# A hybrid retention and sliding-window decoder layer on one core: 28 more 128x512 tiles turned by DMA transposes of two 16-bit planes, in buffers of their own

## The chip, the cores and the metric

One NeuronCore of a Trainium2 chip runs the whole layer in one launch. The metric is the device time of that launch in microseconds (us), the median of several runs. All matrix products are 32-bit: TensorE (PE) takes each fp32 weight tile as a high part and a low part in its reduced fp32 format, and three products make one.

## The reference

The layer is computed for 256 positions of width 2048.

```python
h = modulate(rms_norm(x, norm_ffn1), mod0, mod1)
x = x + 0.5 * mod2 * swiglu(h, w_ffn1_gu, w_ffn1_down)          # d_ff 5632
h = modulate(rms_norm(x, norm_mix), mod3, mod4)
rq, rk, rv, rg, sq, sk, sv, gl_ret, gl_swa = split(h @ w_in)     # 13312 columns
ro = group_rms(retention(rotary(rq), rotary(rk), rv))            # 8 heads, 128 / 256
y_ret = (silu(rg) * ro) @ w_ret_branch
y_swa = sliding_window_attention_with_sinks(sq, sk, sv) @ w_swa_branch   # 32 / 8 heads of 64
x = x + mod5 * ((sigmoid(gl_ret) * y_ret + sigmoid(gl_swa) * y_swa) @ w_out)
h = modulate(rms_norm(x, norm_ffn2), mod6, mod7)
x = x + 0.5 * mod8 * swiglu(h, w_ffn2_gu, w_ffn2_down)
out = rms_norm(x, norm_final)
```

The nine `mod` vectors are `silu(c) @ w_ada + b_ada`, 2048 by 18432 weights that VectorE (DVE) multiplies row by row beside the products ("ada passes", L204).

## The kernel before, in words

Activations are held turned, features on the 128 partitions and the 256 positions along the row, because PE multiplies from that form. A product (`gemm`, L385) makes a chunk of 512 output columns for both halves of the positions in two PSUM banks. It streams the weights in loads of 1 MB (`load`, L309, four buffers in the pool `raws`); each load holds four 128-row blocks and is worked off in two halves. For each half ScalarE (ACT) casts the high part `wh` (L335), DVE subtracts to get the low part `wl` (L336), into a pool of three such pairs, and PE issues twelve 128x512 matmuls (L327, L328, L329). A chunk of a 2048-row product is four loads, eight halves, 96 matmuls.

After each load of a chunk `step` (L300) runs one step of the first generator in the list `side`: a pair of heads of the softmax (`window`, L1000, weights in one step and values in the next) or a head of the retention (L1059). So the softmax and the retention run between the products of the following chunks.

A result of a product has the positions on the partitions. Where a later product needs it, each 128x512 tile of it must be turned. There are two ways in the kernel:

- `transpose_to` (L412): four 128x128 transposes on PE into one PSUM bank (L417) and one copy out of it (L418), by ACT or DVE as the scheduler chooses.
- `turn_by_dma` (L424), which only the feed-forward chunks use, 8 tiles in the first and 20 in the second: ACT copies the low and the high 16 bits of each word apart into two planes (`apart`, L432, two copies), SyncE (SP) issues two DMA transposes (`turn`, L436), and two copies weave the turned planes together (`together`, L442). Planes and turned planes share one tile of the pool `asp` (tile name `a`, two buffers), which the softmax and the products' activation pairs use too. `later` (L552) gives these out over the following loads: the first tile's `apart`, the second's, three empty steps, the first `turn`, the second, then both `together`.

The middle part of the layer, which the change is about, goes in this order: keys and values of the softmax; four chunks of softmax queries (L1012 on, turned into `qo`); two chunks each of rotated queries and keys (L1026 on, into `qk`); four chunks of retention values; the gates of the first half; four chunks of gated retention (L1122 on, into `rot`); then for each half `p` of the columns the two branch products, whose gated sum is turned into `mt` (L1137 on).

SP is the one engine whose order is that of the code: it issues the loads, the ada rows and the DMA transposes in the order in which the kernel calls them, each waiting until its buffer is free. On PE, DVE and ACT a scheduler sets the order when the program is built, and the engine then keeps to it, whatever comes late.

Of the kernel before, what the change touches and what calls it, by code (L numbers as in the profile page):

```python
# [11 lines left out]
U16 = mybir.dt.uint16  # L12
# [5 lines left out]
P = 128  # L18
# [6 lines left out]
CH = 512  # L25
KB = 4
# [51 lines left out]
def layer_kernel(  # L78
# [22 lines left out]
    nc = tc.nc  # L101
# [15 lines left out]
    def nm(s):  # L117
        uid[0] += 1
        return f"{s}_{uid[0]}"
# [7 lines left out]
    def side_bank():  # L127
        return psd.tile([P, CH], F32, tag="pd", name=nm("pd"))
# [7 lines left out]
    def slot():  # L136
        return slots.tile([P, KD * S], F32, tag="slot", name=nm("slot"))
# [201 lines left out]
    def pair_tile():  # L339
        return asp.tile([P, 2, CH], F32, tag="a", name=nm("a"))  # L340
# [42 lines left out]

    def gemm(act, w, col0s, KT=KD):
        banks = [[acc_bank() for _ in range(NT)] for _ in col0s]  # L385
# [27 lines left out]
    def transpose_to(dest, src_of, n, ps=None):  # L413

        ps = ps or bank()
        for j in range(n):
            nc.tensor.transpose(ps[:, j * P : (j + 1) * P], src_of(j), ident)  # L417
        nc.any.tensor_copy(dest, ps[:, : n * P])  # L418

    def words(t):  # L420

        return t.bitcast(U16).rearrange("p (n i) -> p n i", i=2)

    def turn_by_dma(dest, src):  # L424


        both = pair_tile()
        planes = both[:, 0].bitcast(U16).rearrange("p (i n) -> p i n", i=2)
        turned = both[:, 1].bitcast(U16).rearrange("p (i k s) -> p i k s", i=2, k=KB)
        def apart():  # L430
            for i in range(2):
                nc.scalar.copy(planes[:, i, :], words(src)[:, :, i])  # L432

        def turn():
            for i in range(2):
                nc.sync.dma_start_transpose(turned[:, i], planes[:, i, :])  # L436

        into = dest.bitcast(U16).rearrange("p k (s i) -> p k s i", i=2)

        def together():  # L440
            for i in range(2):
                nc.any.tensor_copy(into[:, :, :, i], turned[:, i])  # L442

        return apart, turn, together

# [103 lines left out]
        square_sum(ssq[:, t * 4 + ci : t * 4 + ci + 1], xs)  # L549


    def later(work):  # L552
# [6 lines left out]
        m1()  # L559

    def swiglu_up(banks_g, banks_u, tiles, ci, parts=None, by_dma=False):

        k0 = ci * KB
        dest = tiles[k0 // KD].rearrange("p (k s) -> p k s", s=S)
        kk = k0 % KD
        work = []
        for t in range(NT):
            s = t512()
            g, u = banks_g[t], banks_u[t]
            if parts is not None:  # L570
                nc.vector.tensor_add(s, g, parts[0][t])
                nc.vector.tensor_add(parts[1][t], u, parts[1][t])
                g, u = s, parts[1][t]
            nc.scalar.activation(s, g, AF.Silu)
            nc.vector.tensor_mul(s, s, u)
            if by_dma:
                work.append(turn_by_dma(dest[:, kk : kk + KB, t * P : (t + 1) * P], s))
                continue
            transpose_to(
                dest[:, kk : kk + KB, t * P : (t + 1) * P],  # L580
                lambda j: s[:, j * P : (j + 1) * P],
                KB,
            )
        if work:
            side.append(later(work))

    def ffn_up(held, w, tiles, first, bg=None, turned=()):
        for ci in range(first, DFF // CH):
# [148 lines left out]
    held = Held()  # L737
# [138 lines left out]
    def in_chunk(c0):  # L876
        return gemm(held, wi, [c0])[0]
# [123 lines left out]
    def window(pair):  # L1001
        lg = window_weights(pair)
        yield
        if before:
            window_values(*before.pop())
        before.append((pair, lg))
        if pair == QH // 2 - 1:
            yield
            window_values(*before.pop())
        yield  # L1010

    for ci in range(4):  # L1012
# [12 lines left out]
    qk = slot().rearrange("p (a h s) -> p a h s", a=2, h=RH)  # L1025
    for a, off in ((0, O_RQ), (1, O_RK)):  # L1026
        for ci in range(2):
            b = in_chunk(off + ci * CH)
            for t in range(NT):
# [20 lines left out]
                transpose_to(  # L1050
                    qk[:, a, ci * 4 : ci * 4 + 4, t * P : (t + 1) * P],
                    lambda j: u[:, j * P : (j + 1) * P],
                    4,
                )


    vo = slot().rearrange("p (t n) -> p t n", t=NT)

    def retention(h):  # L1059
        ps = side_bank()  # L1060
        nc.tensor.matmul(
            ps[:, :S], qk[:, 1, h, :P], qk[:, 0, h, :], start=True, stop=True
# [58 lines left out]
    rot = slot().rearrange("p (k s) -> p k s", s=S)  # L1121
    for ci in range(4):  # L1122
        b = in_chunk(O_RG + ci * CH)
        for t in range(NT):
# [3 lines left out]
            transpose_to(  # L1128
                rot[:, ci * 4 : ci * 4 + 4, t * P : (t + 1) * P],
                lambda j: u[:, j * P : (j + 1) * P],  # L1130
                4,
            )

    gate = gate_row()
    mt = slot().rearrange("p (k s) -> p k s", s=S)
# [2 lines left out]
    for p in range(2):  # L1138
        sg = first if p == 0 else gates(p)
        c0s = [(2 * p + i) * CH for i in range(2)]  # L1140
        for g, a, w in ((1, a_swa, w_swa_branch), (0, a_ret, w_ret_branch)):
            banks = gemm(a, w[0], c0s)
            for i in range(2):
                for t in range(NT):
                    nc.vector.tensor_mul(sg[:, g, i, t, :], sg[:, g, i, t, :], banks[i][t])
        for i in range(2):
            for t in range(NT):
                m = sg[:, 0, i, t, :]
                nc.vector.tensor_add(m, m, sg[:, 1, i, t, :])
                k0 = (2 * p + i) * KB  # L1150
                transpose_to(
                    mt[:, k0 : k0 + KB, t * P : (t + 1) * P],
                    lambda j: m[:, j * P : (j + 1) * P],
                    KB,
                )
# [94 lines left out]
```

## Time and profile before

| | |
|---|---|
| median of 3 runs | 2430.84 us (2430.41 to 2431.67) |
| span of the profiled execution, first to last instruction | 2429.6 us |
| what lies around the span, against the median | 1.2 us |
| PE busy | 2385.2 us, 98% |
| DVE busy | 1701.3 us, 70% |
| ACT busy | 1236.0 us, 51% |
| DMA queue q1 | 597.91 MB, 70.8% of the engines' time |
| granted TensorE clock | 0.999 |

The span is one profiled execution; PE, DVE, ACT and SP are engines, PEld is PE's weight load, SPq is SP's queue of DMA issues. A group row gives line, engine, operation, output and inputs by tile name, shape, count, then busy us and mean ns, then the idle time before and what ended it. A matmul row's length contains its latency; how much of PE it takes is read from the starts of the rows that follow each other. The middle part that the change touches stands between about 850 and 1440 us.

### The profile page before, as it was taken

The page shows a single profiled execution, that of the slowest core. Times are in us where ns is not written, and L with a number is a line of the kernel's source. Part 1 is how long each engine was busy: PE and PEld are TensorE (multiplying, and loading weights), DVE is VectorE, ACT ScalarE, POOL GpSimd, SP SyncE. Part 2 cuts the span into 40 slices and gives each one's busy share as a digit, 9 for nine tenths or more (in the row PEclk, how much of TensorE's full clock was granted, in tenths as well). Part 3 has the DMA queues.
Part 4 walks back from the last instruction along what each step waited for, and adds up shares of the span by engine and source line. Part 5 has one row for each costly group of instructions (what it writes and reads, how often), then busy time and mean ns, then how long its engine had stood idle before and what let it go on. Part 6 is the DMA issues. An engine that isn't in the chain of part 4 may idle for free. (4 is left out here: it accounts for less than half of the span.)

```text
span 2429.6 us, 29064 instructions
## 1 busy us (share of the span) xinstructions
PE 2385.2 (98%) x10798; PEld 1946.8 (80%) x10798; DVE 1701.3 (70%) x2735; ACT 1236.0 (51%) x1696; POOL 5.7 (0%) x14
## 2 busy tenths in 40 slices
PE   7999999999999999999999999999999999999998
PEld 4778888888787777788888888887788888888886
DVE  6998777778877677886666776767655555555656
ACT  6544545454545455554544444446554555554544
POOL 0000000000000000000000000000000000000000
PEclk9999999999999999999999999999999999999999
DMA  9987689998875665566676777755677777775563
GB/s 347 341 333 284 217 313 318 356 319 295 311 264 186 243 222 204 206 219 216 233 266 245 251 260 260 279 189 190 215 249 237 243 251 238 248 237 192 185 198 122
DMA packets 274545, 606.43 MB, mean 250 GB/s; under 512 B 40098, under 2 KB 40482, under 8 KB 255586
## 3 DMA queue, kind: packets, MB, share of 16 engines
q1 hardware_dynamic: 272898, 597.91, 70.8%
q0 software_dynamic: 928, 5.61, 0.6%
q8 instruction: 85, 1.39, 0.2%
q10 hardware_dynamic: 576, 1.05, 0.1%
q14 instruction: 58, 0.47, 0.1%
HBM read 595.06 MB, written 2.12 MB: 246 GB/s over the span
## 5 line engine op out<-in xcount | busy, mean ns | idle before, releaser
L336 DVE TENSOR_TENSOR wl<-raw,wh 128x1024 fp32r<-128x1024 f32 (+1 forms) x828 | 995.9, 1208 | 591.2 <-ACT wh L335 585.3
L335 ACT CAST wh<-raw 128x1024 fp32r<-128x1024 f32 (+1 forms) x828 | 861.4, 1042 | 973.0 <-PE pa L328 936.8
L327 PE MATMUL pa<-wh,hh 128*128 128x512 f32 x2224 | 870.5, 393 | 3.4 <-ACT wh L335 2.9
L328 PE MATMUL pa<-wh,hl 128*128 128x512 f32 x2224 | 869.9, 391 | 2.2 <-DVE hl L503 1.8
L329 PE MATMUL pa<-wl,hh 128*128 128x512 f32 x2224 | 798.0, 392 | 4.0 <-DVE wl L336 4.0
L327 PEld LDWEIGHTS pa<-wh,hh 128*128 128x128 f32 x2224 | 418.1, 188 | 93.4 <-ACT wh L335 4.4
L329 PEld LDWEIGHTS pa<-wl,hh 128*128 128x128 f32 x2224 | 415.9, 188 | 95.9 <-DVE wl L336 9.8
L328 PEld LDWEIGHTS pa<-wh,hl 128*128 128x128 f32 x2224 | 418.3, 188 | 89.8 <-DVE hl L503 2.5
L328 PE MATMUL pa<-wh,a 128*128 128x512 f32 x992 | 383.9, 389 | 0.0
L327 PE MATMUL pa<-wh,a 128*128 128x512 f32 x992 | 367.1, 390 | 1.6 <-DVE t L546 1.2
L329 PE MATMUL pa<-wl,a 128*128 128x512 f32 x992 | 367.1, 390 | 0.8 <-DVE wl L336 0.8
L327 PEld LDWEIGHTS pa<-wh,a 128*128 128x128 f32 x992 | 186.1, 188 | 41.5 <-DVE t L546 1.9
L329 PEld LDWEIGHTS pa<-wl,a 128*128 128x128 f32 x992 | 185.9, 188 | 40.6 <-DVE wl L336 2.4
L328 PEld LDWEIGHTS pa<-wh,a 128*128 128x128 f32 x992 | 186.3, 188 | 38.5
L204 DVE CUSTOM_DVE_ANT_0 slot<-slot,cact 128x512 f32<-128x512 f32 (+1 forms) x252 | 192.8, 814 | 10.5 <-DMA slot<-in_w_ada_dram 10.3
L204 DVE CUSTOM_DVE_ANT_0 raw<-raw,cact 128x512 f32<-128x512 f32 (+1 forms) x260 | 167.1, 696 | 42.5 <-DMA raw<-in_w_ada_dram 32.3
L368 DVE TENSOR_TENSOR a<-slot,a 128x512 fp32r<-128x512 f32 x124 | 85.0, 686 | 13.2 <-ACT a L367 13.2
L367 ACT CAST a<-slot 128x512 fp32r<-128x512 f32 x124 | 76.4, 616 | 14.8 <-PE pa L329 14.7
L442 ACT COPY slot<-a 128x512 uint16<-128x512 uint16 x54 | 38.5, 772 | 31.3 <-DMA a<-a 31.3
L204 DVE DVE_READ_ACCUMULATOR2_ANT sums<- 128x1 f32 x512 | 42.4, 83 | 0.0
L418 ACT COPY slot<-ps 128x512 f32<-128x512 f32 x52 | 29.4, 584 | 23.7 <-PE ps L417 23.5
L462 ACT ACTIVATE pd<-x_sb 128x512 f32<-128x512 f32 x32 | 19.0, 593 | 34.6 <-DVE x_sb L547 32.1
(164 smaller groups left out, 1024.2 us busy)
## 6 DMA issues: line engine op xcount, KB each, us to landing
raw<-in_w_ffn_gu_dram SPq DMA_DIRECT2D x152, 1024.0 KB, 5.2
raw<-in_w_in_dram SPq DMA_DIRECT2D x104, 1024.0 KB, 5.0
raw<-in_w_ffn_down_dram SPq DMA_DIRECT2D x88, 1024.0 KB, 5.1
slot<-in_w_ada_dram SPq DMA_DIRECT2D x76, 1024.0 KB, 7.3
raw<-in_w_ada_dram SPq DMA_DIRECT2D x64, 1024.0 KB, 4.8
raw<-in_w_ffn_gu_dram SPq DMA_DIRECT2D x24, 768.0 KB, 6.9
raw<-in_w_swa_branch_dram SPq DMA_DIRECT2D x16, 1024.0 KB, 5.3
raw<-in_w_ret_branch_dram SPq DMA_DIRECT2D x16, 1024.0 KB, 5.1
```

What stands on the lines that cost most here:

```text
L204: nc.vector.tensor_tensor_reduce(out=w[:, at], in0=w[:, at], in1=cact[:, at], scale=1.0, scalar=0.0, op0=ALU.mult, op1=ALU.add, accum_out= ...
L327: nc.tensor.matmul(ps, ah[:, j, ts], wh[:, j, :], start=first, stop=False)
L328: nc.tensor.matmul(ps, al[:, j, ts], wh[:, j, :], start=False, stop=False)
L329: nc.tensor.matmul(ps, ah[:, j, ts], wl[:, j, :], start=False, stop=last)
L335: nc.scalar.copy(hi, src)
L336: nc.vector.tensor_sub(lo, src, hi.bitcast(F32))
L367: nc.scalar.copy(hi, v)
L368: nc.vector.tensor_sub(lo, v, hi.bitcast(F32))
L418: nc.any.tensor_copy(dest, ps[:, : n * P])
L442: nc.any.tensor_copy(into[:, :, :, i], turned[:, i])
L462: nc.scalar.activation(side_bank(), src, AF.Square, accum_out=dest)
```

## The change

Tiles are turned by `turn_by_dma` in 28 more places instead of by `transpose_to`: the 8 tiles of the softmax queries, the 8 of rotated queries and keys, the 8 of gated retention and the 4 of the merged branches of the first half `p = 0`. The second half stays on PE. The planes and the turned planes get two pools of their own, `flat` (4 buffers of 2 KB a partition) and `back` (2 of 2 KB), and are taken when they are written. The scratch space of the GpSimd queue's DMAs is set to 4096 bytes. Turns move out of `side` into a list of their own, `turns`: after each load every generator in it makes one step. The softmax pairs of a chunk are put into `side` only when its tiles are together, eight loads after the chunk's end. In the code behind it, lines stand 15 to 33 further down: the products L327 to L329 become L342 to L344, the cast L335 becomes L350, the load L312 becomes L327, the ada row L199 becomes L201, the weaving copies L442 become L461.

```diff
+    flat = ctx.enter_context(tc.tile_pool(name="flat", bufs=4))
+    back = ctx.enter_context(tc.tile_pool(name="back", bufs=2))
...
+    turns = []
+    def turn_step():
+        for one_turn in list(turns):
+            if next(one_turn, turns) is turns:
+                turns.remove(one_turn)
+    def soon(one_turn):
+        next(one_turn)
+        turns.append(one_turn)
...
     def gemm_part(act, w, col0s, banks, kb, KT):
...
                 tick()
+            turn_step()
...
     def turn_by_dma(dest, src):
-        both = pair_tile()
-        planes = both[:, 0].bitcast(U16).rearrange("p (i n) -> p i n", i=2)
-        turned = both[:, 1].bitcast(U16).rearrange("p (i k s) -> p i k s", i=2, k=KB)
+        held = {}
         def apart():
+            planes = flat.tile([P, 2, CH], U16, tag="flat", name=nm("flat"))
             for i in range(2):
                 nc.scalar.copy(planes[:, i, :], words(src)[:, :, i])
+            held["planes"] = planes
         def turn():
+            turned = back.tile([P, 2, KB, P], U16, tag="back", name=nm("back"))
             for i in range(2):
-                nc.sync.dma_start_transpose(turned[:, i], planes[:, i, :])
+                nc.sync.dma_start_transpose(turned[:, i], held["planes"][:, i, :])
+            held["turned"] = turned
...
+    def later_by_pairs(work):
+        for apart, _, _ in work:
+            apart()
+        for _ in range(5):
+            yield
+        for a in range(0, len(work), 2):
+            for which in (1, 2):
+                yield
+                for parts in work[a : a + 2]:
+                    parts[which]()
...
     for ci in range(4):
         b = in_chunk(O_SQ + ci * CH)
+        work = []
         for t in range(NT):
             u = t512()
             nc.any.tensor_copy(u, b[t])
-            transpose_to(
-                qo[:, ci * 4 : ci * 4 + 4, t * P : (t + 1) * P],
-                lambda j: u[:, j * P : (j + 1) * P],
-                4,
-            )
-        side += [window(pair) for pair in range(ci * 4, ci * 4 + 4)]
+            work.append(turn_by_dma(qo[:, ci * 4 : ci * 4 + 4, t * P : (t + 1) * P], u))
+        pairs = range(ci * 4, ci * 4 + 4)
+        soon(later(work, lambda pairs=pairs: side.extend(window(pair) for pair in pairs)))
```

The rotated queries and keys and the gated retention change in the same way, with `soon(later(work))`; the merged branches use `soon(later_by_pairs(work))`.

On PE the place is the first chunk of rotated keys, second load. Before, the four transposes of a tile of rotated queries (`t_7822`, into the bank `ps_7829`) stand between the products of that chunk (`pa_7848` and `pa_7849` are its two banks):

```order
L327 MATMUL pa_7848<-wh_7916,hh_4122 128x512
L328 MATMUL pa_7848<-wh_7916,hl_4123 128x512
L329 MATMUL pa_7848<-wl_7917,hh_4122 128x512
L327 MATMUL pa_7849<-wh_7916,hh_4122 128x512
L417 MATMUL ps_7829<-small_c,t_7822 128x128 x4
L328 MATMUL pa_7849<-wh_7916,hl_4123 128x512
L329 MATMUL pa_7849<-wl_7917,hh_4122 128x512
L327 MATMUL pa_7848<-wh_7935,hh_4122 128x512
L328 MATMUL pa_7848<-wh_7935,hl_4123 128x512
```

Now, at the same load of that chunk (banks `pa_7693` and `pa_7694`):

```order
L344 MATMUL pa_7693<-wl_7756,hh_4136 128x512
L344 MATMUL pa_7694<-wl_7756,hh_4136 128x512
L342 MATMUL pa_7693<-wh_7755,hh_4136 128x512
L343 MATMUL pa_7693<-wh_7755,hl_4137 128x512
L344 MATMUL pa_7693<-wl_7756,hh_4136 128x512
L342 MATMUL pa_7694<-wh_7755,hh_4136 128x512
L343 MATMUL pa_7694<-wh_7755,hl_4137 128x512
L344 MATMUL pa_7694<-wl_7756,hh_4136 128x512
L342 MATMUL pa_7693<-wh_7774,hh_4136 128x512
```

The transposes are gone from PE and the products follow each other.

On SP the place is the loads of the second chunk of rotated keys (`raw` from `in_w_in`) with the ada rows between them. Before:

```order
L312 DMA raw_8119<-in_w_in_dram 128x4x512
L199 DMA raw_8137<-in_w_ada_dram 128x2048
L312 DMA raw_8186<-in_w_in_dram 128x4x512
L312 DMA raw_8241<-in_w_in_dram 128x4x512
L199 DMA raw_8276<-in_w_ada_dram 128x2048
L312 DMA raw_8308<-in_w_in_dram 128x4x512
```

Now (`flat_7730` and `flat_7793` hold the planes of the two tiles of rotated queries, `back_8064` and `back_8137` take them turned):

```order
L327 DMA raw_7968<-in_w_in_dram 128x4x512
L201 DMA raw_7986<-in_w_ada_dram 128x2048
L327 DMA raw_8029<-in_w_in_dram 128x4x512
L454 DMA_TRANSPOSE back_8064<-flat_7730 128x4x128 x2
L327 DMA raw_8099<-in_w_in_dram 128x4x512
L201 DMA raw_8134<-in_w_ada_dram 128x2048
L454 DMA_TRANSPOSE back_8137<-flat_7793 128x4x128 x2
L327 DMA raw_8160<-in_w_in_dram 128x4x512
```

Two pairs of transposes now stand between the loads; the loads and ada rows keep their order.

On ACT the place is the same tile's way into `qk`. Before, one copy out of PSUM (`slot_7305` is `qk`) stands among the casts and the softmax's copies:

```order
L335 CAST wh_7916<-raw_7914 128x1024
L418 COPY t_7802<-ps_7803 128x384
L418 COPY t_7808<-ps_7809 128x384
L335 CAST wh_7935<-raw_7914 128x1024
L335 CAST wh_7973<-raw_7971 128x1024
L997 COPY slot_6378<-ps_7814 128x256
L418 COPY slot_7305<-ps_7829 128x4x128
L335 CAST wh_7990<-raw_7971 128x1024
```

Now (`slot_7142` is `qk`; the other of the two weaving copies of this tile stands on DVE, and its two `apart` copies stand a few rows further up):

```order
L350 CAST wh_7844<-raw_7825 128x1024
L989 ACTIVATE a_7796,sm_7814<-a_7796,ng_7809 128x128 x2
L989 ACTIVATE a_7796,sm_7814<-a_7796,ng_7809 128x256 x2
L1030 COPY slot_6392<-ps_7745 128x256
L983 ACTIVATE se_7811<-se_7811 128x4
L350 CAST wh_7886<-raw_7884 128x1024
L461 COPY slot_7142<-back_8064 128x4x128
L350 CAST wh_7903<-raw_7884 128x1024
L350 CAST wh_7970<-raw_7968 128x1024
L434 COPY t_7864<-ps_7865 128x384
L434 COPY t_7870<-ps_7871 128x384
L350 CAST wh_7989<-raw_7968 128x1024
```

The copy that waited for PE is replaced by a copy that waits for a transfer, one cast behind the cast `wh_7844` of the load whose buffer `raw_8029` takes (the fourth `raw` back on SP).

More of the change, by code (lines that the diff above doesn't have):

```diff
@@ L441, in together @@
             for i in range(2):
-                nc.any.tensor_copy(into[:, :, :, i], turned[:, i])
+                nc.any.tensor_copy(into[:, :, :, i], held["turned"][:, i])
         return apart, turn, together
@@ L549, in add_gated, with later @@
         square_sum(ssq[:, t * 4 + ci : t * 4 + ci + 1], xs)
-    def later(work):
+    def later(work, then=None):
         (a0, t0, m0), (a1, t1, m1) = work
@@ L559, in later @@
         m1()
+        if then is not None:
+            then()
+    def later_by_pairs(work):
[8 more added lines that the diff above has]
+                    parts[which]()
     def swiglu_up(banks_g, banks_u, tiles, ci, parts=None, by_dma=False):
@@ L584, in swiglu_up @@
         if work:
-            side.append(later(work))
+            turns.append(later(work))
     def ffn_up(held, w, tiles, first, bg=None, turned=()):
@@ L1028, in layer_kernel @@
             b = in_chunk(off + ci * CH)
+            work = []
             for t in range(NT):
@@ L1049, in layer_kernel @@
                 nc.vector.tensor_add(u4[:, :, 1, :], u4[:, :, 1, :], v4[:, :, 1, :])
[L1050 to L1053, printed above, removed]
+                work.append(
+                    turn_by_dma(qk[:, a, ci * 4 : ci * 4 + 4, t * P : (t + 1) * P], u)
                 )
+            soon(later(work, lambda heads=(a, ci): kept.add(heads)))
     vo = slot().rearrange("p (t n) -> p t n", t=NT)
     def retention(h):
+        assert {(0, h // 4), (1, h // 4)} <= kept
         ps = side_bank()
@@ L1123, in layer_kernel @@
         b = in_chunk(O_RG + ci * CH)
+        work = []
         for t in range(NT):
@@ L1127, in layer_kernel @@
             nc.vector.tensor_mul(u, u, vo[:, t, ci * CH : (ci + 1) * CH])
[L1128 to L1132, printed above, removed]
+            work.append(turn_by_dma(rot[:, ci * 4 : ci * 4 + 4, t * P : (t + 1) * P], u))
+        soon(later(work))
     gate = gate_row()
@@ L1141, in layer_kernel @@
         for g, a, w in ((1, a_swa, w_swa_branch), (0, a_ret, w_ret_branch)):
+            assert g == 1 or not turns
             banks = gemm(a, w[0], c0s)
@@ L1145, in layer_kernel @@
                     nc.vector.tensor_mul(sg[:, g, i, t, :], sg[:, g, i, t, :], banks[i][t])
+        work = []
         for i in range(2):
@@ L1150, in layer_kernel @@
                 k0 = (2 * p + i) * KB
[L1151 to L1155, printed above, removed]
+                dest = mt[:, k0 : k0 + KB, t * P : (t + 1) * P]
+                if p == 0:
+                    work.append(turn_by_dma(dest, m))
+                    continue
+                transpose_to(dest, lambda j: m[:, j * P : (j + 1) * P], KB)
+        if work:
+            soon(later_by_pairs(work))
     gate_load(gate, 5)
@@ L1227 @@
     from concourse.bass_utils import run_bass_kernel_spmd as _run
[L1229 removed]
+    nc = _bacc.Bacc("TRN2", target_bir_lowering=False, num_devices=1, dynamic_dma_scratch_size=4096)
     arrays, args = {}, []
```

2 lines of the change are left out of this document (1 added, 1 removed).

## The prediction

> **What bounds the kernel now.** I read the page's busy times and slices first, then three stretches, then the starts of single rows on PE, ACT and SP, and last what ACT waited for.
>
> ```profile
> PE 2385.2 (98%) x10798; PEld 1946.8 (80%) x10798; DVE 1701.3 (70%) x2735; ACT 1236.0 (51%) x1696; POOL 5.7 (0%) x14
> ...
> PEclk9999999999999999999999999999999999999999
> ```
>
> PE works 98% of the span at the full granted clock, so whatever leaves PE's queue leaves the time, as long as PE stays fed. The stretches show where it is fed (columns: us; busy us and count on PE, PEld, DVE, ACT, POOL; clock; DMA share; GB/s):
>
> ```profile
> 875.00:1110.00 235.00, 235.00 (x1283) 187.03 (x1282) 181.47 (x410) 132.42 (x282) 0.00 (x0) 1.00 0.59 206
> 1190.00:1430.00 240.00, 239.25 (x1073) 197.30 (x1073) 162.36 (x245) 113.74 (x129) 0.00 (x0) 1.00 0.72 255
> 1760.00:2180.00 420.00, 420.00 (x1855) 347.77 (x1854) 235.67 (x285) 214.05 (x251) 1.59 (x3) 1.00 0.76 241
> ```
>
> The first is the softmax with the queries and keys, the second the gated retention and the first branches, both touched by the change. The third is the second feed-forward, which turns its tiles by transfer already: 1855 matmuls in 420.00 us, 0.2264 us each, which is a matmul's bare pitch (below). So **PE lost nothing there to 19 turned tiles** (38 transposes, two a tile). All three stretches are bound by PE; a busy PE can hide pauses of up to the 0.16 us by which a row is longer than its pitch, so the terms below come from starts.
>
> **The change, part by part: what leaves PE.** A tile's four transposes between two products:
>
> ```profile
> 886.77 0.40 PE L328 MATMUL pa<-wh,hl 128*128 128x512 f32 x1
> 887.00 0.39 PE L329 MATMUL pa<-wl,hh 128*128 128x512 f32 x1
> 887.23 0.40 PE L327 MATMUL pa<-wh,hh 128*128 128x512 f32 x1
> 887.46 0.39 PE L328 MATMUL pa<-wh,hl 128*128 128x512 f32 x1
> 887.69 0.39 PE L329 MATMUL pa<-wl,hh 128*128 128x512 f32 x1
> 887.92 0.60 PE L417 MATMUL ps<-small_c,t 128*128 128x128 f32 x4
> 888.28 0.47 PE L327 MATMUL pa<-wh,hh 128*128 128x512 f32 x1
> 888.59 0.39 PE L328 MATMUL pa<-wh,hl 128*128 128x512 f32 x1
> ```
>
> Undisturbed products start 0.23 us apart (886.77, 887.00, 887.23). From the product at 887.69 to the second one behind the transposes, at 888.59, it is 0.90 us instead of 2 x 0.227 = 0.454. A tile thus costs PE 0.446 us: 0.36 us from the first transpose to the next product, and the rest because that product is slow to get under way. The tiles are 8 + 8 + 8 + 4 = 28, and 28 x 0.446 = **12.5 us** leave PE.
>
> The Trainium skill (VectorE: DVE Perf Modes, The three transpose paths) gives a 128x128 transpose 390 ns on TensorE; by that, 112 of them would be 43.7 us. The trace's rows are shorter and overlap: four take 0.36 us of PE. The measurement decides.
>
> **What ACT gets.** Means of one, from the groups by shape:
>
> ```profile
> L442 ACT COPY slot<-a 128x512 uint16<-128x512 uint16 x54 | 38.5, 772 | 31.3 <-DMA a<-a 31.3
> ...
> L432 ACT COPY a<-t 128x512 uint16<-128x512 uint16 x56 | 30.6, 617 | 1.1 <-DVE t L575 0.9
> L418 ACT COPY slot<-ps 128x512 f32<-128x512 f32 x52 | 29.4, 584 | 23.7 <-PE ps L417 23.5
> ```
>
> A tile adds 2 x 0.617 + 2 x 0.772 - 0.584 = 2.19 us of ACT. In the first stretch 14 tiles' copies go (the group L418 has 14 there), so 14 x 2.19 = 30.7 us more. A copy that weaves planes also waits for its transfer with all casts behind it in ACT's queue, and PE waits for those casts. What ACT waited for in the first stretch, and in the feed-forward:
>
> ```profile
> ACT wh L335 <- PE pa L328: 52.2, 39, 2.4
> ACT slot L418 <- PE ps L417: 15.1, 10, 3.2
> ```
>
> ```profile
> ACT wh L335 <- PE pa L328: 161.8, 103, 1.7
> ACT slot L442 <- DMA a<-a: 30.4, 17, 3.5
> ```
>
> A cast that waits for PE is ACT's lead: 52.2 us, and the 15.1 us for PE's transposes end with them, 67.3 us in all. Against it stand 30.7 us of copies and, at the feed-forward's 30.4 / 19 = 1.6 us a tile, 22.4 us of waits: 53.1. So **14.2 us of 235 remain: enough on average, thin in places.** Were that cover gone, every further us would be PE's.
>
> **The thin places.** The transfers' way in the feed-forward:
>
> ```profile
> 1840.20 1.06 ACT L335 CAST wh<-raw 128x1024 fp32r<-128x1024 f32 x1 [1.66 <-PE pa L328]
> ...
> 1840.38 3.84 SPq L436 DMA_TRANSPOSE a<-a  x2
> ...
> 1842.92 1.06 ACT L335 CAST wh<-raw 128x1024 fp32r<-128x1024 f32 x1 [1.66 <-PE pa L328]
> ...
> 1844.01 1.23 DVE L336 TENSOR_TENSOR wl<-raw,wh 128x1024 fp32r<-128x1024 f32 x1 [1.49 <-ACT wh L335]
> ...
> 1845.64 1.06 ACT L335 CAST wh<-raw 128x1024 fp32r<-128x1024 f32 x1 [1.66 <-PE pa L328]
> ...
> 1848.48 1.40 ACT L442 COPY slot<-a 128x512 uint16<-128x512 uint16 x2 [1.78 <-DMA a<-a]
> ```
>
> The first transpose needed 8.1 us from issue (1840.38) to use (1848.48), and in that time three casts went by, 2.72 us apart: the pace of twelve products, that is PE's time for half a load. SP can issue a pair only behind the load before it in the code, and that load waits until its buffer is read. In the order shown, `back_8064` is weaved only one cast behind that point. From the start of the cast `wh_7844` it takes 1.06 (cast) + 1.23 (subtraction) + 0.4 (the load's issue, 1839.96 to 1840.38) + 8.1 + 0.77 (weaving) + 1.06 (the next cast) = 12.6 us. PE then holds three halves, plus the one cast between, 4 x 2.72 = 10.9 us, and the softmax's matmuls of one pair, up to some 2 us. So PE loses 0 to 1.7 us there. Two more places stand as close (`back_7587` with one cast between, and `back_10382`, whose two weaving copies both stand on DVE). Bounds for all thin places: 0 (the feed-forward's row) and 3 x 1.7 = 5.1; I take **2.2 us**, nearer to the feed-forward, since it is the same mechanism.
>
> ```profile
> 1839.96 0.37 SPq L312 DMA_DIRECT2D raw<-in_w_ffn_gu_dram  x1
> ```
>
> **What I cost at nothing.** *SP*: a pair of transposes holds its queue 3.84 us (the row at 1840.38), less than the 5.44 us of a load's work, and it runs three loads ahead; without that lead a pair would cost up to 3.84 us. *Gated retention and merged branches* (12 tiles, 26 us more ACT): there casts waited 117.8 us for PE in 240. *The burst at the merge*, eight copies of 0.617 = 4.9 us at once, is under the 8.2 us of three halves. *The softmax starts eight loads later*: 48 steps of softmax and retention have 52 loads left before the gated retention needs them; short of that, each missing step would cost a load's 5.4 us or so. *Tables*: retention now runs among the sigmoid gates, four more loads of ACT's table at 1.28 us, beside casts that wait for PE. *Planes of their own*: the feed-forward's order hardly moves. *The smaller GpSimd scratch*: POOL is busy 5.7 us in the whole span. *DMA*: the engines are 59% busy in the first stretch, and 76% where transfers go unnoticed.
>
> ```profile
> ACT wh L335 <- PE pa L328: 117.8, 79, 3.6
> ```
>
> ```profile
> L1115 ACT ACT_TABLE_LOAD x3 | 3.8, 1283 | 0.1
> ```
>
> **The sum** against the profiled execution: 2429.6 - 12.5 + 2.2 = 2419.3 us of span; the median of before is 1.2 us above its span, so **2420.5 us**, 0.4% faster. With no stall it is 2418.3.
>
> **Rivals.** *ACT starves PE* (the other side). Mechanism: the weaving copies wait at the head of ACT's queue, in the softmax stretch, where the lead is 67.3 us and the copies take 30.7. The point from which PE pays is (67.3 - 30.7) / 14 = 2.6 us of wait a tile. At 3.5 us (the longest wait above, on every tile) the loss is 14 x 3.5 + 30.7 - 67.3 = 12.4 us and the gain is gone: 2430.7. Beyond 3.9 us a tile it is slower by over 0.2%; at 4.5 us, 26.4 us are lost: 2444.7. For it: only one or two casts stand between issue and use at some tiles, ada rows mix into SP's queue, and ACT has exponentials to catch up with. Against it: the feed-forward's average of 1.6. *Half of it*: PE loses 4 to 9 us in thin places, for instance also where DVE weaves; 2422.5 to 2427, on both sides of the edge of what counts as faster. *The transfers stand on PE's path*: if nothing else hid them and each of 28 tiles cost PE the 8.1 us above, 227 us more, 2645. The Trainium skill (VectorE: DVE Perf Modes, Rules for kernel authors) would keep 128x128 transposes on TensorE when PSUM may take them, and its table has 1309 ns for the DMA's. The 420.00 us with 19 such tiles and nothing lost speak against that here. *The change does nothing*: excluded but for the scheduler putting other small work into PE's queue in new pieces.
>
> **How the numbers follow.** Forecast (2418 to 2423): 0.58. Half of it: 0.22, of which about 0.12 below 2426. ACT starves PE: 0.17, about 0.04 of it still within 0.2%. On PE's path 0.01, nothing 0.02. A measurement of this kernel can tell about 0.2%, 4.9 us, from no change. Faster by over 0.2% (under 2426.0): 0.58 + 0.12 = 0.70. Within: 0.10 + 0.04 + 0.02 = 0.16. Slower (over 2435.7): 0.13 + 0.01 = 0.14. The range starts at 2416.5, the case without a stall and 1.8 us for side effects of the new order; it ends at 2434, into the starving case up to a wait of 3.7 us a tile, which leaves out some 0.15 above and little below.
>
> **What would show it.** Right: the group of transposes from tile `t` loses 96 of its 176, that from `slot` 16 of 32; matmuls start 0.227 us apart over the first two stretches but for softmax and retention; ACT's waits for DMA grow by about 45 us and its casts' waits for PE shrink to some 15 us in the softmax stretch. Wrong: PE rows with `wh L335` or `wl L336` as releaser of over 1 us beside weaving copies in 900 to 1100 us, waits for DMA of over 3 us a tile, or a fall of PE's clock.

## The result, and the profile after

The changed kernel takes **2432.30 us** (median of 12 runs, 2430.14 to 2435.01), the kernel before 2431.49 us beside it (12 runs, 2430.17 to 2434.15). The ratio is 1.0002, with a 95% interval of 0.9994 to 1.0010: the forecast 0.4% is not there, and no difference can be told. The profiled execution's span is 2430.4 us against 2429.6.

PE did lose the 112 transposes (10798 matmuls became 10686), but its busy time fell by 6.1 us only. From the page of the changed kernel:

```profile
PE 2379.1 (98%) x10686; PEld 1936.6 (80%) x10686; DVE 1706.3 (70%) x2751; ACT 1274.9 (52%) x1768; POOL 5.6 (0%) x14
```

The three stretches that the prediction showed, now (the same columns: busy us and count on PE, PEld, DVE, ACT, POOL; clock; DMA share; GB/s):

```profile
875.00:1110.00 235.00, 230.31 (x1191) 179.53 (x1192) 186.02 (x425) 145.53 (x307) 0.00 (x0) 1.00 0.73 220
1190.00:1430.00 240.00, 237.12 (x1041) 193.97 (x1041) 166.23 (x274) 131.39 (x168) 0.00 (x0) 1.00 0.79 258
1760.00:2180.00 420.00, 419.97 (x1854) 347.33 (x1853) 235.27 (x285) 213.88 (x252) 1.58 (x3) 1.00 0.78 241
```

In the softmax stretch PE was never seen idle before; now it stands 4.7 us of 235. The gated stretch lost 2.1 us of busy time as well. The feed-forward, third, is as it was. The clock is full throughout.

What ACT waited for, in the first of these stretches and in the second (us in total, times, longest):

```profile
ACT slot L461 <- DMA back<-flat: 43.2, 13, 6.3
ACT wh L350 <- PE pa L343: 21.8, 17, 1.7
```

```profile
ACT wh L350 <- PE pa L343: 82.0, 53, 3.2
ACT slot L461 <- DMA back<-flat: 20.1, 7, 5.9
```

So on average ACT's lead had not run out (casts still waited 21.8 us for PE), and yet PE waited. One place shows how. It is the timeline of the changed kernel, engines ACT, SP and PE; rows of other work between these are left out:

```profile
936.49 3.13 SPq L454 DMA_TRANSPOSE back<-flat  x2
938.02 1.06 ACT L350 CAST wh<-raw 128x1024 fp32r<-128x1024 f32 x1 [0.70 <-PE pa L343]
944.35 1.40 ACT L461 COPY slot<-back 128x512 uint16<-128x512 uint16 x2 [5.28 <-DMA back<-flat]
945.62 1.04 ACT L350 CAST wh<-raw 128x1024 fp32r<-128x1024 f32 x1
...
948.33 2.50 SPq L454 DMA_TRANSPOSE back<-flat  x2
...
948.67 1.05 ACT L350 CAST wh<-raw 128x1024 fp32r<-128x1024 f32 x1
...
953.46 0.39 PE L344 MATMUL pa<-wl,hh 128*128 128x512 f32 x1
953.87 0.77 ACT L461 COPY slot<-back 128x512 uint16<-128x512 uint16 x1 [4.14 <-DMA back<-flat]
...
954.50 1.03 ACT L350 CAST wh<-raw 128x1024 fp32r<-128x1024 f32 x1
...
955.59 0.50 PE L342 MATMUL pa<-wh,hh 128*128 128x512 f32 x1 [1.74 <-ACT wh L350]
```

Between the issue of a tile's transposes (936.49) and its weaving copies (944.35) stands **one** cast in ACT's queue; the copies then hold the queue for 5.28 us, with the next cast behind them. The second tile does it again for 4.14 us, and at 953.46 PE has used up what was cast: its next product starts 2.13 us later.

To see where time is won and lost, I numbered the 9984 products (the matmuls of L327 to L329, now L342 to L344) and compared the starts of the same number in both traces. Number 3456 is ahead of the first turned query tile, 4992 behind the softmax and the retention, 5376 behind the gated tiles' turns, in the first branch product, and 5760 behind the merged tiles' turns, in the gates that follow. Change of time between these numbers against the kernel before, in us:

| | to 4992 | to 5376 | to 5760 | to the end |
|---|---|---|---|---|
| by the forecast, without stalls | -7.1 | -3.6 | -1.8 | 0 |
| changed kernel | **+2.8** | **0.0** | -2.1 | +0.4 |

The gain is lost in the first two parts: 9.9 and 3.6 us. Behind 5760, where the change has nothing, the profiled executions of the runs below also take 0.4 to 2.0 us longer than the kernel before's, so a difference of that size in one execution should not be read. The first part can be split further. Its 1536 products take 0.227 us each; what the part takes beyond that is idle time of over 0.15 us ahead of a matmul, or the small matmuls of softmax and retention (time from product to product around them, less the pitch), or the transposes (likewise; in a mixed group each is given what it takes alone), or products that start late by less than 0.15 us:

| us | idle | softmax and retention | transposes | products | sum |
|---|---|---|---|---|---|
| before | 0.0 | 45.0 | 14.3 | 8.3 | 67.5 |
| changed | 4.7 | 47.5 | 9.3 | 8.8 | 70.3 |

Transposes and products together should have fallen by 7.1 us and fell by 4.5. Idle time is 4.7 us, and **softmax and retention cost 2.5 us more** for the same matmuls.

### The profile page after: what moved, and what is told of

Same layout as the page of the kernel before. It is cut to its first block, busy times and chain, and to the rows that moved or that the text cites. A ratio compares the mean times of both kernels' runs of the same rounds, so it can differ in the third digit from the quotient of the medians.

```text
span 2430.4 us, 28951 instructions
## 1 busy us (share of the span) xinstructions
PE 2379.1 (98%) x10686; PEld 1936.6 (80%) x10686; DVE 1706.3 (70%) x2751; ACT 1274.9 (52%) x1768; POOL 5.6 (0%) x14
## 5 line engine op out<-in xcount | busy, mean ns | idle before, releaser
L350 ACT CAST wh<-raw 128x1024 fp32r<-128x1024 f32 (+1 forms) x828 | 858.8, 1040 | 889.3 <-PE pa L343 866.7
L342 PE MATMUL pa<-wh,hh 128*128 128x512 f32 x2224 | 870.3, 393 | 5.4 <-ACT wh L350 4.8
L344 PE MATMUL pa<-wl,hh 128*128 128x512 f32 x2224 | 795.9, 392 | 6.8 <-DVE wl L351 6.7
L344 PEld LDWEIGHTS pa<-wl,hh 128*128 128x128 f32 x2224 | 414.6, 188 | 101.2 <-DVE wl L351 14.7
L342 PEld LDWEIGHTS pa<-wh,hh 128*128 128x128 f32 x2224 | 417.9, 188 | 96.4 <-ACT wh L350 6.8
L342 PE MATMUL pa<-wh,a 128*128 128x512 f32 x992 | 367.5, 390 | 2.1 <-DVE t L565 1.2
L344 PE MATMUL pa<-wl,a 128*128 128x512 f32 x992 | 366.8, 390 | 0.8 <-DVE wl L351 0.8
L342 PEld LDWEIGHTS pa<-wh,a 128*128 128x128 f32 x992 | 185.9, 188 | 42.9 <-DVE t L565 1.9
L344 PEld LDWEIGHTS pa<-wl,a 128*128 128x128 f32 x992 | 186.1, 188 | 40.9 <-DVE wl L351 2.7
L461 ACT COPY slot<-back 128x512 uint16<-128x512 uint16 x100 | 71.5, 770 | 104.3 <-DMA back<-flat 104.2
L448 ACT COPY flat<-t 128x512 uint16<-128x512 uint16 x104 | 57.4, 618 | 10.4 <-DVE t L1082 6.2
```

Source lines behind the costliest of these rows:

```text
L342: nc.tensor.matmul(ps, ah[:, j, ts], wh[:, j, :], start=first, stop=False)
L344: nc.tensor.matmul(ps, ah[:, j, ts], wl[:, j, :], start=False, stop=last)
L350: nc.scalar.copy(hi, src)
L461: nc.any.tensor_copy(into[:, :, :, i], held["turned"][:, i])
```

## The experiments

Two causes were on the table. First, weaving copies wait at the head of ACT's queue for the landing, and PE starves. Second, the softmax, which starts eight loads later, is laid out worse in PE's queue. Against them: ACT's extra copies cost by their own work; the fuller DMA delays loads and rows; copies that stand on DVE delay the subtractions. Differences below are against the kernel before, run beside each.

**Weaving late.** In the middle part both weaving copies go to ACT, behind the newest weight cast (`newest["cast"]`, kept where casts are made):

```diff
+                with tc.issue_after(newest["cast"].ins):
+                    for i in range(2):
+                        nc.scalar.copy(into[:, :, :, i], held["turned"][:, i])
```

> The changed kernel, but in the middle part (queries, rotated, gated retention, merged) a turned tile's two weaving copies are both ACT's and stand behind the newest weight cast at the place where the code gives them out, so that the transfers have long landed. The theory (the weaving copies wait at the head of ACT's queue and PE starves, some 8 us; another 5 us are lost by the softmax that starts eight loads later): ACT's waits for landing transfers in 875 to 1110 us fall from 43 us to under 10, PE's pauses over 0.15 us there from 4.7 us to about 1, and the time falls by 4 to 9 us against the changed kernel, to 2423-2428. Rival 1 (ACT's added copies themselves cost the time, not their waits): the copies are as many, so no change, 2431-2434. Rival 2 (the DMA is fuller, loads and rows land later): traffic is the same, no change, and the pauses stay with DMA or subtractions as releasers.

Measured: 2424.48 us against 2431.67, ratio 0.9972 (0.9959 to 0.9984), 7.8 us under the changed kernel's median. Six to nine casts now stand between issue and weaving copy of a query or key tile. First stretch, busy times, then the largest of ACT's waits, among which none for a landing is left:

```profile
875.00:1110.00 235.00, 235.00 (x1235) 185.30 (x1233) 190.53 (x430) 157.21 (x323) 0.00 (x0) 1.00 0.71 232
```

```profile
ACT wh L351 <- PE pa L344: 54.2, 45, 1.8
ACT a L995 <- DVE ng L981: 8.6, 9, 1.6
```

PE's idle time there is gone, with *more* work on ACT (157.21 us against 145.53) and the same transfers: neither the copies' own work nor the DMA was the loss (weight loads of `w_in` land in 5.5 us, 5.6 in the changed kernel, 5.0 before).

**The softmax late, all turns on PE.** The kernel before, with `side.extend(window(pair) ...)` eight loads later:

```diff
-        side += [window(pair) for pair in range(ci * 4, ci * 4 + 4)]
+        waiting.append([8, range(ci * 4, ci * 4 + 4)])
```

> The kernel before, all turns on TensorE, but each group of softmax pairs is handed out eight loads later, as in the changed kernel. Theory (the later start alone makes the small matmuls dearer, as fewer pairs run side by side): 3 to 6 us slower than before, 2434-2437, with the softmax's matmuls costing PE some 5 us more. Rival (the later start costs nothing, all of the loss is ACT's waits): within 1 us of before. Rival (the lost 5 us belong to the disturbed order of casts and copies, not to the start): within 1 us too, told apart from the former by the run that weaves late.

Measured: 2434.36 against 2431.67, ratio 1.0010 (1.0001 to 1.0018), 2.7 us slower, just under the 3 to 6 expected. Up to product 4992 it loses 2.0 us, and the small matmuls cost 2.1 us more: the second cause is real, at less than half of the 5 us that I had given it. What such a cost can consist of shows in the starts on PE. Before, a pair's twelve value matmuls and its eight scores in a row:

```profile
898.64 0.39 PE L327 MATMUL pa<-wh,hh 128*128 128x512 f32 x1
898.96 0.44 PE L985 MATMUL ps<-t,slot 128*64 128x128 f32 x4
899.23 0.61 PE L990 MATMUL ps<-t,slot 128*64 128x128 f32 x8
899.76 0.49 PE L917 MATMUL pd<-slot,slot 64*128 64x128 f32 x4
900.09 0.60 PE L921 MATMUL pd<-slot,slot 64*128 64x256 f32 x4
900.62 0.50 PE L328 MATMUL pa<-wh,hl 128*128 128x512 f32 x1
```

In the changed kernel, the same twenty, with two scores put behind the values:

```profile
965.16 0.39 PE L344 MATMUL pa<-wl,hh 128*128 128x512 f32 x1
965.48 0.50 PE L950 MATMUL pd<-slot,slot 64*128 64x128 f32 x4
965.81 0.59 PE L954 MATMUL pd<-slot,slot 64*128 64x256 f32 x2
966.33 0.44 PE L1018 MATMUL ps<-t,slot 128*64 128x128 f32 x4
966.60 0.61 PE L1023 MATMUL ps<-t,slot 128*64 128x128 f32 x8
967.14 0.70 PE L954 MATMUL pd<-slot,slot 64*128 64x256 f32 x2
967.76 0.50 PE L342 MATMUL pa<-wh,hh 128*128 128x512 f32 x1
```

From product to product 1.98 us became 2.60: the scores use half of the array's rows, and four of them in one piece take less than twice two.

**Gated retention and merged branches alone**, the queries and keys back on `transpose_to`:

```diff
-            work.append(turn_by_dma(qo[:, ci * 4 : ci * 4 + 4, t * P : (t + 1) * P], u))
+            transpose_to(qo[:, ci * 4 : ci * 4 + 4, t * P : (t + 1) * P], lambda j: u[:, j * P : (j + 1) * P], 4)
```

> The changed kernel with only the gated retention (8 tiles) and half of the merged branches (4 tiles) turned by transfers, queries and keys on TensorE as before. Saved on PE 12 x 0.446 = 5.4 us. Theory: 3.6 us of the 8 tiles' gain is lost again to waiting weaving copies, the merged branches keep theirs, so 1 to 2.5 us faster than before, about 2429.5. Rival (no stall outside the softmax stretch, as the prediction had it): 5.4 us faster, 2426. Rival (the whole loss lies here): slower than before by over 2 us.

Measured: 2428.80 against 2431.67, ratio 0.9988 (0.9980 to 0.9997). By product starts -2.1 us in the gated part (3.6 forecast) and -2.1 up to 5760: somewhat better than the theory, less than the prediction.

**Rotated, gated and merged, late**, the queries on PE (and the weaving as in the late run):

```diff
+        side += [window(pair) for pair in range(ci * 4, ci * 4 + 4)]
-        soon(later(work, lambda pairs=pairs: side.extend(window(pair) for pair in pairs)))
```

> Rotated queries and keys, gated retention and half of the merged branches by transfers (20 tiles, 20 x 0.446 = 8.9 us off PE), the softmax's queries on TensorE so that the softmax starts as early as in the kernel before, and the weaving copies late on ACT. Theory: neither the waits nor the late start are left, so 6 to 9 us faster than before, 2422-2425. Rival 1 (ACT's copies themselves cost): 12 of 28 parts of the loss are gone at most, so 0 to 4 us faster. Rival (fuller DMA): little of the gain, 0 to 4 us faster, with pauses released by DMA.

Measured: 2426.28 against 2431.67, ratio 0.9978 (0.9968 to 0.9987), 5.4 us faster, short of the theory's 6 to 9. To 4992 it gains 2.4 of 3.6 us and to 5376 all of 3.6, but from there to 5760 it gains only 0.2 of 1.8: two pauses stand in the branch products at 1351 and 1367 us, 0.73 us released by the split of the activation (`a`), 0.77 us by `wl`. The last gated tiles are woven late and used at once; the late run loses the same 1.8 us there.

**The wait taken away.** The weaving copies read the flat planes; this leaves out the use of the turned data, while transfers and copies stay:

```diff
-                nc.any.tensor_copy(into[:, :, :, i], held["turned"][:, i])
+                nc.any.tensor_copy(into[:, :, :, i], held["planes"][:, i].rearrange("p (k s) -> p k s", k=KB))
```

> The changed kernel, but the weaving copies read the flat planes, not the turned ones: it leaves out the use of the turned data, while the transfers, all copies and their places stay. Theory (the wait for the landing is what costs): as in the run that weaves late, 6 to 10 us faster than the changed kernel, 2422-2426, with PE's pauses gone from 875 to 1110 us. Rival (the copies' own time, or their place in the queue ahead of a cast, costs without any wait): 2429-2433.

Measured: 2428.14 against 2431.45, ratio 0.9986 (0.9977 to 0.9995): 4.2 us under the changed kernel, outside the 6 to 10 expected and outside the rival's span too. Idle time in the first part fell from 4.7 to 1.1 us, but the scheduler, given new dependences, split the softmax's matmuls further (28 groups between products instead of 23), and softmax and retention cost 48.0 us. The wait explains its share; the order of the small matmuls kept the rest.

**Both weaving copies on ACT, at their old place:**

```diff
-                nc.any.tensor_copy(into[:, :, :, i], held["turned"][:, i])
+                nc.scalar.copy(into[:, :, :, i], held["turned"][:, i])
```

> The changed kernel with both weaving copies of a middle tile always on ACT, but at the place where the changed kernel has them. It tells the place from the engine, which the late run both changed: 4 of 32 copies of the softmax stretch stand on DVE in the changed kernel. Theory (the place decides): ACT still waits some 40 us for landings in 875 to 1110 us, and the time is within 2.5 us of the changed kernel, 2430-2435. Rival (copies on DVE delay the subtractions, and that was the loss): 4 to 8 us faster than the changed kernel, 2424-2428.

Measured: 2435.22 against 2431.45, ratio 1.0017 (1.0008 to 1.0026), 2.9 us above the changed kernel's median and a little beyond the theory's span, with ACT's waits for landings as they were:

```profile
ACT slot L462 <- DMA back<-flat: 41.2, 13, 5.2
```

So the late run's gain came from the place, not from the engine: with all copies on ACT at the old place nothing is won.

**The weaving copies two loads later in the code**, for queries and rotated tiles. `later` makes one step a load, so two empty steps are two loads (2 x 5.44 = 10.9 us), not the two half loads of 5.4 us that the expectation names:

```diff
-        for f in (a0, a1, None, None, None, t0, t1, m0):
+        for f in (a0, a1, None, None, None, t0, t1, None, None, m0):
```

> The changed kernel, with the weaving copies of queries and rotated tiles given out two half loads (5.4 us) later in the code; the engine is the scheduler's choice as before. Theory (a wait of 3 us a tile at the head of the queue): 5.4 us take nearly all of it away, ACT's waits for landings in 875 to 1110 us fall from 43 us to under 10, 5 to 9 us faster than the changed kernel, 2423-2427; the softmax starts a load later still, for under 1 us. Rival (the landing itself slides with the place, because the transposes wait for something that the place moves as well): waits and time as in the changed kernel.

Measured: 2434.65 against 2431.45, ratio 1.0012 (1.0003 to 1.0021). My theory's number failed here:

```profile
ACT slot L461 <- DMA back<-flat: 39.0, 13, 5.0
```

The reason is not the rival's (the transposes did not slide): the copies did not move. In ACT's queue one cast or none stood between issue and weaving at 13 of the 16 tiles of queries and keys in the changed kernel, and at 14 here. The scheduler placed the copies by a reckoning of its own, and calling them two loads later in the code did not change that.

**Late for queries and rotated tiles alone.** The late run, with its choice switched off for the two other kinds of tile (`False` is the argument `late`):

```diff
-            work.append(turn_by_dma(rot[:, ci * 4 : ci * 4 + 4, t * P : (t + 1) * P], u))
+            work.append(turn_by_dma(rot[:, ci * 4 : ci * 4 + 4, t * P : (t + 1) * P], u, False))
...
-                    work.append(turn_by_dma(dest, m))
+                    work.append(turn_by_dma(dest, m, False))
```

> The changed kernel with late weaving (behind the newest weight cast, on ACT) for queries and rotated tiles alone; gated retention and merged tiles weave as in the changed kernel. From the starts of PE's products: to the end of the softmax as the late run (6.7 us ahead of before), behind it as the run with gated and merged tiles alone (4.1 us more up to the merged branches' end). Sum: 2420-2422, 9.5 to 11 us faster than before, some 3 us faster than the late run. Rival (the gated retention's stalls come with what the softmax leaves behind, not with its own weaving): as the late run, 2424-2425.

Measured: 2424.07 against 2431.45, ratio 0.9971 (0.9960 to 0.9982). To 4992 it is the late run again (-6.3 us against -6.3); the gated part gains nothing (+0.1, against -2.1 in the run with gated and merged tiles alone). My sum of two runs' parts missed by 3 us: the gated tiles' waits depend on what stands around them. The time is the rival's, but by luck: behind 4992 the late run wins 2.5 us in the gated part and nothing up to 5760, this run nothing and 1.7 us.

**The dose between.** As the late run, but behind the cast four places earlier:

```diff
-                with tc.issue_after(newest["cast"].ins):
+                with tc.issue_after(casts[-5].ins):
```

> The run that weaves late, but with the weaving copies behind the weight cast that stands four casts (10.9 us) ahead of the newest one: two or three casts between a transfer's issue and its use, where the changed kernel has one and the late run six to nine. It is the dose between the two, by place alone. Theory (what counts is how many casts of ACT's queue stand between issue and weaving copy): a landing of 5.6 us is covered by two or three casts of 2.7 us, so ACT's waits for landings in 875 to 1110 us fall from 43 us to under 15, and the time is 5 to 8 us under the changed kernel, 2424-2427. Rival (the order of the softmax's small matmuls in TensorE's queue is what the late run really improved): the time follows that order's cost, 31.9 us in the late run and 34.1 in the changed kernel, and not the waits; with an order as in the changed kernel 2429-2432 in spite of short waits.

Measured: **2423.75** against 2431.69, ratio 0.9968 (0.9957 to 0.9980), the lowest median, though not to be told from the 2424.07 and 2424.48 of the runs that weave later. Three to six casts, not the two or three expected, stand between issue and weaving copy of a query or key tile, and no wait for a landing is left in either stretch. ACT's largest waits and busy times in the first, then the busy times in the second:

```profile
ACT wh L351 <- PE pa L344: 45.0, 34, 2.7
ACT a L995 <- DVE ng L981: 17.9, 8, 4.2
```

```profile
875.00:1110.00 235.00, 234.73 (x1227) 184.72 (x1226) 188.56 (x429) 154.64 (x321) 0.00 (x0) 1.00 0.75 231
...
1190.00:1430.00 240.00, 239.18 (x1055) 196.97 (x1054) 169.31 (x277) 136.18 (x176) 0.00 (x0) 1.00 0.81 266
```

The rival holds for a small share only. By its own measure the softmax's small matmuls cost 32.8 us, between the late run and the changed kernel. Of the 7.3 us by which the first part is shorter than in the changed kernel, 4.4 are idle time, 1.6 transposes and products, and 1.3 the small matmuls of softmax and retention. The run also keeps the merged branches' gain (2.3 us up to 5760), which the late run gave away.

**Rotated queries and keys alone, at their old place.** Of the changed kernel only these lines stay, the queries (as above), the gated and the merged tiles (as below) go back to `transpose_to`:

```diff
+                work.append(
+                    turn_by_dma(qk[:, a, ci * 4 : ci * 4 + 4, t * P : (t + 1) * P], u)
                 )
+            soon(later(work, lambda heads=(a, ci): kept.add(heads)))
```

> The kernel before with the rotated queries and keys alone turned by transfers (8 tiles, 3.6 us off TensorE), woven where the changed kernel weaves them; the softmax starts as early as in the kernel before. It has the waits without the later start. Theory (a weaving copy one cast behind its issue waits some 3 us, and PE pays about half a us a tile; the small matmuls keep their order): 3.6 us are saved and 3 to 4.5 lost in pauses, so within 1.5 us of before, 2430-2433. Rival (all is lost through the softmax's later start): 3 to 4 us faster than before, 2427.5-2428.5.

Measured: 2429.56 against 2431.69, ratio 0.9993 (0.9984 to 1.0002), a little better than the theory's span. There were no pauses at all; ACT waited little:

```profile
ACT slot L461 <- DMA back<-flat: 9.1, 6, 2.2
```

And yet only 1.6 of 3.6 us came through up to 4992: softmax and retention cost 1.4 us more, although the softmax started at its old place. The run did not hold the place, though: five of its eight tiles have two casts between issue and weaving copy, where one of the same eight has two in the changed kernel. So it does not show what waits at the old place cost by themselves. It does show that the small matmuls can become dearer by other edits than a late start.

**Queries and rotated tiles alone:**

```diff
-            work.append(turn_by_dma(rot[:, ci * 4 : ci * 4 + 4, t * P : (t + 1) * P], u))
-        soon(later(work))
+            transpose_to(rot[:, ci * 4 : ci * 4 + 4, t * P : (t + 1) * P], lambda j: u[:, j * P : (j + 1) * P], 4)
...
-                if p == 0:
+                if False:
```

> The changed kernel with the queries and the rotated tiles alone turned by transfers; gated retention and merged branches stay on TensorE. Theory (the loss sits in the softmax stretch, and the parts add up): 7.1 us saved and 9.8 lost, 2 to 4 us slower than before, 2433.5-2435.5; with the run of the other half (2.9 faster) it gives the changed kernel. Rival (the halves disturb each other): equal to or faster than before.

Measured: 2433.90 against 2431.69, ratio 1.0008 (1.0000 to 1.0017): 2.2 us slower, with 38.7 us of waits for landings. Together with the other half (2.9 faster) that gives -0.7, and the changed kernel stands at +0.8: the parts add up to within 1.5 us, in part by luck: up to 4992 this run loses only 1.0 us against the changed kernel's 2.8, and 1.5 us stand behind 5760.

The pieces of the first part side by side (us; one profiled execution each, so about 1 us in a piece should not be believed):

| | idle | softmax, retention | transposes | products | sum | median, difference to before |
|---|---|---|---|---|---|---|
| before | 0.0 | 45.0 | 14.3 | 8.3 | 67.5 | |
| changed | 4.7 | 47.5 | 9.3 | 8.8 | 70.3 | +0.8 |
| softmax late, turns on PE | 0.0 | 47.1 | 13.9 | 8.6 | 69.5 | +2.7 |
| two loads later | 4.1 | 48.4 | 9.3 | 8.3 | 70.0 | +3.2 |
| all on ACT, old place | 2.7 | 47.8 | 8.8 | 9.4 | 68.7 | +3.8 |
| wait taken away | 1.1 | 48.0 | 8.7 | 8.1 | 66.0 | -3.3 |
| four casts sooner | 0.3 | 46.2 | 8.8 | 7.7 | 63.0 | -7.9 |
| late | 0.0 | 45.4 | 9.0 | 6.9 | 61.2 | -7.2 |

## Why the prediction was wrong

- *What leaves PE, 12.5 us:* right to within a tenth. Where nothing waits (the late run), transposes and products fell by 6.7 us for 16 tiles, 0.416 us a tile against 0.446; for 28 tiles that would be 11.6.
- *ACT's lead, 14.2 us spare of 67.3:* right as an average and useless as a bound. Casts still waited 21.8 us for PE, while copies waited 43.2 us instead of 22.4: 3.1 us a tile, not the feed-forward's 1.6.
- **The failed step: "The thin places", 2.2 us, bounds 0 to 5.1.** I read one order of ACT's rows in detail, counted three places with one cast or none between, and let the feed-forward's average stand for the rest. In the trace 13 of the 16 query and key tiles have one cast or none; in the second feed-forward 8 of 20 tiles have one, the others two, but there the casts had 161.8 us of lead in 420, against 52.2 in 235 here. The measured term is some 7 us in the first part (4.7 idle, and the 2.2 by which transposes and products cost more than in the late run, if all of it is hidden waiting) and up to 3.6 in the gated part: about 10.
- *"The softmax starts eight loads later", at nothing:* wrong. I counted steps and asked whether they suffice, not in which order the scheduler would lay the pieces on PE. It was 2.5 us here, and 2.1 with all turns on PE. But the late run starts its softmax just as late and pays 0.4: what costs is the order that the scheduler came to in each build, not the late start as such.
- *SP, DMA, merged branches, tables, scratch at nothing:* nothing of the loss was found there. DMA is 73% busy in the first stretch, the merged tiles kept their 1.8 us.
- *The rival "ACT starves PE"*, 17%, was nearest: it named the mechanism, the stretch and, for 3.5 us a tile, 2430.7 us. The stated range holds the measured time only because it was drawn out to 2434 for this rival. Its break-even of 2.6 us a tile came from the average lead, and so counts on what single places do not have.
- *The signs:* the transposes from `t` fell from 176 to 80 and those from `slot` from 32 to 16, as said. The casts' waits for PE in the softmax stretch fell from 52.2 to 21.8 us, where some 15 was said. ACT's waits for DMA grew by 72.9 us (31.3 to 104.2), not 45. Both signs for "wrong" appeared: a PE row of 1.74 us released by `wh`, and over 3 us of wait a tile.

By its table the Trainium skill (VectorE: DVE Perf Modes, Rules for kernel authors) keeps 128x128 transposes on TensorE where PSUM may take them. For the change as it was made this holds, since nothing was won; woven late, the same transfers win 0.3%, and the measurement decides. The 390 ns that the prediction quotes from the Trainium skill (VectorE: DVE Perf Modes, The three transpose paths) are given there for bf16; the tiles here are fp32.

What stays open: how much of the 2.5 us of order could be had back, since no run fixed PE's order while it changed only the waits; and why the gated tiles' waits differ between runs that weave them alike.

## What to carry to other kernels

When a copy that waits for a transfer joins a queue that feeds the bound engine, count for *each* tile how many instructions stand between issue and use, and give it as many as the landing takes. Here the two transposes of a query or key tile landed 5 to 9 us after the first one's issue; with three to six casts between, 2.7 us apart or more, ACT waited for none of them; in the changed kernel, with mostly one or none, it waited 3.1 us a tile. Whether PE feels the wait depends on the lead as well: in the second feed-forward one cast was enough for 8 of 20 tiles. A lead that suffices on average does not cover single places. And check in the built order that a later call did move the instruction, and that other work on the bound engine did not change its order.

## What the runs showed of the hardware

Matmuls that use half of the array's rows cost by how they stand. Eight scores of a pair in one piece take 0.95 us between products. In the run with the wait taken away one pair's scores stood as four separate twos: 0.51, 0.62, 0.82 and 0.83 us, 2.78 in all. The Trainium skill (TensorE: Matmul & The Clock Gate, Part 3: Packing small matmuls) lets matmuls in different row groups run at once, and the rows agree: the four L921 above take from 900.09 to 900.62, while two L954 by themselves take from 967.14 to 967.76. The starts of the single matmuls show why. The kernel keeps one head of a pair in the first 64 partitions and the other in the last 64. In one piece the L921 start two at a time (900.09 and 900.10, then both at 900.31); the split twos belong to one head each and start one behind the other (967.14, then 967.46).
